# FFN 2 of a macaron layer: quarters' differences taken from PSUM by VectorE, and a pair job's sum taken from its PSUM bank

## The chip, the cores and the metric

The kernel runs on one core of a Trainium2 chip. The metric is the device time of one execution in microseconds. The kernel before takes 1099.75 us, the median of three runs (1099.45 to 1100.01).

The core's engines work side by side, each through its own list of instructions in order, and wait for one another by semaphores: TensorE (PE in the profile) multiplies and writes to PSUM, VectorE (DVE) and ScalarE (ACT) read PSUM and SBUF, GpSimd (POOL) reads SBUF here, and DMAs are issued from SyncE's queue (SP) and POOL's.

## The reference

One layer over 512 tokens of width 1024, in float32: a half-step SwiGLU FFN, a mixer (a recurrent branch and a windowed attention, merged by gates), and a second half-step FFN, each between RMS norms. The part that matters here is the end of the mixer and the first half of FFN 2:

```python
h = h + rms_norm(merged @ w_o[l], mix_post_g[l])
f = swiglu(rms_norm(h, ffn2_pre_g[l]), ffn2_w1[l], ffn2_w3[l], ffn2_w2[l])
h = h + 0.5 * rms_norm(f, ffn2_post_g[l])
```

with `swiglu(x, w1, w3, w2) = (silu(x @ w1) * (x @ w3)) @ w2` and 2816 hidden columns.

## The kernel before

**Precision.** Every float32 operand is held as a high part (a copy rounded to the type float32r) and a low part (what the rounding left), and a product is three matmuls: high by high, high by low, low by high. Making the two parts is called a split here. It is a copy on ScalarE and a subtraction on VectorE (L226 and L227, helper split2): `whi`, `wlo` of weights, `Xh`, `Xl` and the two planes of the tile uT of activations.

**Strassen jobs.** FFN 2's matrix x^T (1024 by 512) lies in quarters: two halves of its features by two halves of its tokens. The first two column tiles of w1 and w3 (128 hidden columns each) are multiplied plainly. The other 20 run in pairs, w1 and w3 in turn: 20 pair jobs (class Pairs, names w1b and w3b, jobs 0 to 19), each with seven block products instead of eight by Winograd's form of Strassen's method. The quarters and four combinations of them are the moving operands:

- b11, b21 and b22 are quarters, as uT holds them;
- t1 = x01 - x00, t2 = x11 - t1, t3 = x11 - x01, t4 = x10 - t2, where x01 is the first half of the features and the second half of the tokens. t1 to t3 are split into slots of SBUF (to_slots), t4 into uT in place of x01 (to_uT).

A job's weights are two raw tiles (a11, a12 and a21, a22). POOL makes the sums S12 (s1, s2) and S34 (s3, s4) of them, four instructions of 512 columns a job (L1038, L1039, L1033, L1034). A job's splits are: the first raw tile, S12, S34 (1024 columns each) and a22 (512). They are made one job ahead, within the previous job: method prep, steps 1 to 4, and step 0 for POOL's sums, two jobs ahead.

**A job's order on PE and what takes its banks.** Each product is 12 matmuls of 128x256. With its three PSUM banks bu, bx and bc a job runs: a11*b11 into bu (copied to q1 by ScalarE, L1083), s1*t1 into bx (copied to q5, L1086), then a22*t4 of the *job before* into that job's own bu, s2*t2 added into bu (copied to u, L1094), a12*b21 into bc (VectorE adds q1, L1106), s4*b22 added into bx (VectorE adds u, L1111), and s3*t3 added into bu. That last sum is the lower right quarter: ScalarE copies bu to v (L1117) and VectorE adds q5 to v (L1118). Then a22*t4 goes on in the same bu, two products later. Every second job (w3) multiplies its results by the silu of those of the job before (L1128, L1129, L1146); the silu (L1141 to L1143) is ScalarE's.

VectorE's order in a job is: split of the next job's first raw tile, split of S12, adds at L1106 and L1111, split of S34, add at L1118, products (in w3's jobs), split of a22.

**The hand-over into FFN 2.** tok_gemm ends the mixer: for each of four tiles of 128 tokens it normalizes, transposes by PE into two PSUM banks (one for each half of the features), and ScalarE and VectorE split the banks into uT (transpose_out, L370 and L372). Beside that, ScalarE copies the unsplit values of all four tiles to four slots xf (transpose_xf, L380), the first two tiles' early, the last two's after the last tile's split. The hook `then` (operands) now runs: a table load for silu, t1 by VectorE from two xf slots and its split, t2 and its split, t3 by POOL; t4 by VectorE (L1998) after it. PE meanwhile multiplies the four plain tiles.

**Slots.** All tiles of SBUF come from one pool of 42 slots, handed out as earlier users release theirs. So what an instruction waits for can be a reader of the slot's earlier tile on any engine.

Of the kernel before, what the change touches and what calls it, by code (L numbers as in the profile page):

```python
# [12 lines left out]
AF = mybir.ActivationFunctionType  # L13
ALU = mybir.AluOpType

P = 128
SEQ = 512
D = 1024
# [8 lines left out]
EPS = 1e-6  # L27
# [24 lines left out]
def hybrid_layer(ctx: ExitStack, tc: tile.TileContext, a: dict, out: bass.AP):  # L52
    nc = tc.nc
    act, dve, pool, pe, sp = nc.scalar, nc.vector, nc.gpsimd, nc.tensor, nc.sync
# [169 lines left out]
    def split2(hi, lo, src):  # L224

        act.activation(hi, src, AF.Copy)  # L226
        dve.tensor_tensor(out=lo, in0=src, in1=f32(hi), op=ALU.subtract)  # L227
# [15 lines left out]
    def unit(nm, i, **kw):  # L243
        w = get(nm, i)
        ps = bank("f")
        mm_feat(ps, w, **kw)
        return ps
# [116 lines left out]
    def transpose_out(banks, t, xf=None, parts=(0, 1)):  # L364
        c = slice(t * P, (t + 1) * P)
        for half, ps in enumerate(banks):
            ks = slice(half * 4, half * 4 + 4)
            v = ps.rearrange("p (k c) -> p k c", k=4)
            if 0 in parts:
                act.activation(uT[:, 0, ks, c], v, AF.Copy)  # L370
            if 1 in parts:
                dve.tensor_tensor(out=uT[:, 1, ks, c], in0=v, in1=f32(uT[:, 0, ks, c]), op=ALU.subtract)  # L372
        if xf:
            transpose_xf(banks, t, xf)

    def transpose_xf(banks, t, xf, halves=(0, 1)):
        for half in halves:
            ps = banks[half]
            v = ps.rearrange("p (k c) -> p k c", k=4)
            act.activation(xf[half, t // 2][:, :, (t % 2) * P : (t % 2 + 1) * P], v, AF.Copy)  # L380


    def tok_gemm(nm, xs, n, R, gpost_name, scale, gpre_name, first, x_to=None, xf=None, spill=False, then=None, eps=D * EPS, pre=None, at_=None, g=None):

# [12 lines left out]
        x_to = x_to or (lambda k: None)  # L397
# [20 lines left out]
        g, us, trs = g or [], {}, {}  # L418
# [122 lines left out]
        t = NT - 1  # L541
# [34 lines left out]
            start(range(1))  # L576
        trs[t] = transpose_mm(us[t])
        transpose_out(trs[t], t)
        transpose_xf(trs[t - 1], t - 1, xf)
        transpose_xf(trs[t], t, xf)  # L580
        if then:
            then()
        if not pre:
# [407 lines left out]
    class Pairs:  # L991
# [75 lines left out]
        def run(self, tail, hooks={}):  # L1067
# [4 lines left out]
            for n, (nm, f) in enumerate(self.jobs):  # L1072
                W = self.w.pop(n)
                first = nm == self.na
                tmp = slot([P, 4, 256], name="ct")
                q1, q5, u, v = (tmp[:, i, :] for i in range(4))
                c = slot([P, 2, SEQ], name="cc")
                if first:
                    self.c1[f] = c
                bu, bx, bc = (bank("c")[:, :256] for _ in range(3))  # L1080
# [33 lines left out]
                silu = lambda: None  # L1114
                mm_s(W["s3"], X["t3"], bu, True)
                del W["s3"], W["s4"]
                act.activation(v, bu, AF.Copy)  # L1117
                dve.tensor_tensor(out=c[:, 1, 256:], in0=v, in1=q5, op=ALU.add)  # L1118
                if n == len(self.jobs) - 1:
                    tail()  # L1120
                    if self.R is not None:
# [214 lines left out]
    ps = [bank("f") for _ in range(NS)]  # L1336
# [385 lines left out]
    for i in range(8):  # L1722
        ps = unit("wg", i)
# [16 lines left out]
    for i in range(2):  # L1740
        ps = unit("wk", i)
# [8 lines left out]
    for t in range(NT):  # L1750
        ps = bank("v")
        c = slice(t * P, (t + 1) * P)
        o = ps[:, :256]
# [20 lines left out]
    for i in range(2):  # L1774
        ps = unit("wq", i)
# [135 lines left out]
    for nm, i in att_units:  # L1911
        w = w_first or get(nm, i)
        w_first = None
        ps = bank("f")
# [32 lines left out]
    hid, tn = Hidden(TAIL_B, GS_B), []  # L1947
    X2 = {"b11": uview(0, 0), "b21": uview(1, 0), "b22": uview(1, 1)}
# [3 lines left out]
    gw = []  # L1952
# [21 lines left out]
    for at_, fn in zip(MARKS_W, (lambda n: split_to(k_w + len(TS_AT) + n + 1), h_back)):  # L1974
        for n, u in enumerate(at_):
            hooks_w[u].append(lambda n=n, fn=fn: fn(n))
    xf = {(hh, th): slot([P, 4, 256], name="xf") for hh in range(2) for th in range(2)}
    def operands():
        act.activation(small(4, "tiny")[:, 0:1], vec[:, 0:1], AF.Silu)
        t = [slot([P, 4, 256], name="T") for _ in range(4)]  # L1980
        tn.extend(t)
        dve.tensor_tensor(out=t[0], in0=xf[0, 1], in1=xf[0, 0], op=ALU.subtract)
        X2["t1"] = to_slots(t[0])
        dve.tensor_tensor(out=t[1], in0=xf[1, 1], in1=t[0], op=ALU.subtract)
        X2["t2"] = to_slots(t[1])
        pool.tensor_tensor(out=t[2], in0=xf[1, 1], in1=xf[0, 1], op=ALU.subtract)
        pairs_b.prep(1, 0)

    rubbish.append(slot([P, D], name="junk"))
    bs = tok_gemm(  # L1990
        "wo", mixed, KT, len(TAIL_W), "mix_post_g", 1.0, "ffn2_pre_g",
        [("w1b", 0), ("w3b", 0), ("w1b", 1), ("w3b", 1)], xf=xf, spill=True, then=operands, eps=4.0 * D * EPS, pre=half_w,
        at_=(0, 2, 3, XW_AT), g=gw)
    half_w = mixed = hooks_w = None
    rubbish.clear()

# [11 lines left out]
    X2 = pairs_b = None  # L2008
# [58 lines left out]
XW_AT = (1, 2, 3, 4)  # L2067
# [59 lines left out]
```

## Time and profile before

| What | Value |
|---|---|
| Median of three runs | 1099.75 us |
| The profiled execution's own time | 1099.81 us |
| Its span, first to last instruction | 1098.0 us |
| Mean granted clock of TensorE | 0.999 |
| First matmul of the pair jobs | 782.1 us after the span's start |
| Busy in 780 to 800 us: PE, DVE, ACT, POOL | 20.00, 19.76, 12.29, 19.68 us |
| Busy in 860 to 880 us: PE, DVE, ACT, POOL | 20.00, 18.71, 10.74, 12.63 us |

The times of the trace count from the start of the span. 1.81 us of the execution lie around the span. A row of a timeline has its start, its duration, engine, line, operation, output and inputs, and in brackets the idle time of the engine ahead of it with what ended that. A duration on VectorE contains the time in which the instruction stands in the engine and does not get on. Matmuls of 256 columns follow each other every 0.12 us and overlap, so their rows are longer (0.28) than their distance.

### The profile page before, as it was taken

How to read it: one execution, taken by the hardware profiler on the slowest of the kernel's cores; microseconds unless marked ns; L12 is line 12 of the kernel's file. 1: busy time of each engine (PE TensorE's matmuls, PEld its weight loads, DVE VectorE, ACT ScalarE, POOL GpSimd, SP SyncE). 2: the span in 40 equal slices, each digit the busy share in tenths (PEclk: the TensorE clock that was granted, in tenths of full speed). 3: DMA queues.
4: the chain of work that ended last, by engine and by line, in shares of the span. 5: the costliest groups of instructions: out<-in, count | busy, mean ns of one | idle time of the engine just before them, and what ended most of it. 6: DMA issues, size and time to landing. Idle time of an engine off the chain costs nothing.

```text
span 1098.0 us, 18217 instructions
## 1 busy us (share of the span) xinstructions
PE 1087.7 (99%) x6880; PEld 986.1 (90%) x6880; DVE 930.4 (85%) x1345; ACT 715.4 (65%) x1241; POOL 405.9 (37%) x366
## 2 busy tenths in 40 slices
PE   9999999999999999999999999999999999999997
PEld 7899999998889878899888888888999999998886
DVE  5987999989997998887778866877899989889996
ACT  7756555598767778666656666457555455578872
POOL 0144933232102613242444443111877656633200
PEclk9999999999999999999999999999999999999999
DMA  9325663389866652156222347676423323449923
GB/s 335 126 84 141 126 154 114 105 189 229 235 166 221 155 156 64 39 192 229 66 90 79 120 138 201 170 254 161 147 78 116 105 88 111 145 102 243 211 74 135
DMA packets 56361, 161.72 MB, mean 147 GB/s; under 512 B 5696, under 2 KB 7616, under 8 KB 56272
## 3 DMA queue, kind: packets, MB, share of 16 engines
q1 hardware_dynamic: 39104, 117.77, 31.7%
q0 software_dynamic: 16880, 42.25, 19.7%
q8 instruction: 54, 0.88, 0.3%
q10 hardware_dynamic: 288, 0.52, 0.1%
q14 instruction: 35, 0.29, 0.1%
HBM read 144.81 MB, written 13.62 MB: 144 GB/s over the span
## 4 chain that ended last, share of the span: by engine, by line
PE 96%; DVE 2%; ACT 1%; issue 1%; DVEq 0%; POOL 0%; ACTq 0%; POOLq 0%
PE c L986 13%; PE c L985 13%; PE c L987 13%; PE f L237 9%; PE f L239 9%; PE f L238 9%; PE hw L857 7%; PE hw L856 7%; PE hw L855 7%; PE pt L1850 1%; PE hw L257 1%; PE hw L255 1%; PE hw L256 1%; PE s L1814 1%; PE s L1813 1%
## 5 line engine op out<-in xcount | busy, mean ns | idle before, releaser
L986 PE MATMUL c<-uT,wlo 128*128 128x256 f32 x516 | 146.1, 283 | 1.3 <-DVE wlo L227 1.3
L987 PE MATMUL c<-uT,whi 128*128 128x256 f32 x516 | 146.0, 283 | 0.0
L985 PE MATMUL c<-uT,whi 128*128 128x256 f32 x516 | 146.0, 283 | 0.0
L986 PE MATMUL c<-Xh,wlo 128*128 128x256 f32 x504 | 142.7, 283 | 0.5 <-DVE wlo L227 0.5
L985 PE MATMUL c<-Xh,whi 128*128 128x256 f32 x504 | 142.7, 283 | 0.0
L237 PE MATMUL f<-uT,whi 128*128 128x512 f32 (+1 forms) x392 | 140.7, 359 | 0.1
L238 PE MATMUL f<-uT,wlo 128*128 128x512 f32 (+1 forms) x392 | 139.1, 355 | 0.0
L239 PE MATMUL f<-uT,whi 128*128 128x512 f32 (+1 forms) x392 | 139.0, 355 | 0.0
L987 PE MATMUL c<-Xl,whi 128*128 128x256 f32 x456 | 129.0, 283 | 0.0
L227 DVE TENSOR_TENSOR wlo<-S,whi 128x1024 fp32r<-128x1024 f32 x86 | 122.5, 1426 | 4.1 <-ACT whi L226 2.0
L226 ACT ACTIVATE whi<-S 128x1024 fp32r<-128x1024 f32 x86 | 88.6, 1055 | 30.4 <-DVE S L1034 28.7
L986 PEld LDWEIGHTS c<-uT,wlo 128*128 128x128 f32 x516 | 99.0, 192 | 1.7 <-DVE wlo L227 1.5
L985 PEld LDWEIGHTS c<-uT,whi 128*128 128x128 f32 x516 | 99.0, 192 | 0.2
L987 PEld LDWEIGHTS c<-uT,whi 128*128 128x128 f32 x516 | 99.0, 192 | 0.0
L986 PEld LDWEIGHTS c<-Xh,wlo 128*128 128x128 f32 x504 | 96.7, 192 | 0.7 <-DVE wlo L227 0.7
L985 PEld LDWEIGHTS c<-Xh,whi 128*128 128x128 f32 x504 | 96.8, 192 | 0.3 <-issue 0.3
L857 PE MATMUL hw<-whi,uT 128*128 128x512 f32 x228 | 88.7, 389 | 0.0
L855 PE MATMUL hw<-whi,uT 128*128 128x512 f32 x228 | 88.7, 389 | 0.0
L987 PEld LDWEIGHTS c<-Xl,whi 128*128 128x128 f32 x456 | 87.5, 192 | 0.0
L237 PEld LDWEIGHTS f<-uT,whi 128*128 128x128 f32 x392 | 74.1, 189 | 11.8 <-issue 1.4
L856 PE MATMUL hw<-wlo,uT 128*128 128x512 f32 x216 | 84.0, 389 | 0.0
L239 PEld LDWEIGHTS f<-uT,whi 128*128 128x128 f32 x392 | 74.1, 189 | 10.5
(453 smaller groups left out, 3202.4 us busy)
## 6 DMA issues: line engine op xcount, KB each, us to landing
raw_w3a<-in_w3a_dram SPq DMA_DIRECT2D x21, 512.0 KB, 4.6
raw_w1a<-in_w1a_dram SPq DMA_DIRECT2D x20, 512.0 KB, 4.4
raw_w1b<-in_w1b_dram SPq DMA_DIRECT2D x20, 512.0 KB, 4.2
raw_w3b<-in_w3b_dram SPq DMA_DIRECT2D x20, 512.0 KB, 4.2
raw_w2a<-in_w2a_dram SPq DMA_DIRECT2D x17, 512.0 KB, 6.5
raw_wg<-in_wg_dram SPq DMA_DIRECT2D x16, 512.0 KB, 3.5
raw_w2a<-in_w2a_dram POOLq DMA_DIRECT2D x15, 512.0 KB, 10.4
raw_w2b<-in_w2b_dram SPq DMA_DIRECT2D x15, 512.0 KB, 8.2
```

Of the source, the lines that this page charges most:

```text
L226: act.activation(hi, src, AF.Copy)
L227: dve.tensor_tensor(out=lo, in0=src, in1=f32(hi), op=ALU.subtract)
L237: pe.matmul(ps[:, c0:c1], wh[:, s], h_, start=k == 0 and c0 == 0, stop=False, skip_group_check=True)
L238: pe.matmul(ps[:, c0:c1], wl[:, s], h_, start=False, stop=False, skip_group_check=True)
L239: pe.matmul(ps[:, c0:c1], wh[:, s], l_, start=False, stop=k == KT - 1, skip_group_check=True)
L255: pe.matmul(acc[n], x[:, 0, c], wh[:, s], start=first, stop=False, skip_group_check=skip)
L855: pe.matmul(ps, xs[:, 0, j, c], hi[:, j, :], start=start and j == 0, stop=False, skip_group_check=True)
L856: pe.matmul(ps, xs[:, 0, j, c], lo[:, j, :], start=False, stop=False, skip_group_check=True)
L857: pe.matmul(ps, xs[:, 1, j, c], hi[:, j, :], start=False, stop=i == self.G - 1, skip_group_check=True)
L985: pe.matmul(ps, wh[:, s], xh, start=first, stop=False, skip_group_check=True)
L986: pe.matmul(ps, wl[:, s], xh, start=False, stop=False, skip_group_check=True)
L987: pe.matmul(ps, wh[:, s], xl, start=False, stop=k == 3, skip_group_check=True)
```

## The change

There are two edits. The first is at the hand-over. The slots xf for the last two token tiles go. tok_gemm gets a hook diff; after the last tile's split, VectorE subtracts straight from the four transposed banks of the last two tiles: t1 from the bank of the first half of the features and x00, t2 from the bank of the second half and t1. t3 is now t2 - x00, the same value, and is made by VectorE instead of POOL. ScalarE's last four copies go. The second is in Pairs.run, for the jobs of FFN 2 alone (self.R is None): no copy to v; VectorE's add reads the bank bu itself.

```diff
+        if diff:
+            diff(t - 1, trs[t - 1])
+            diff(t, trs[t])
+        else:
+            transpose_xf(trs[t - 1], t - 1, xf)
+            transpose_xf(trs[t], t, xf)
...
-                act.activation(v, bu, AF.Copy)
-                dve.tensor_tensor(out=c[:, 1, 256:], in0=v, in1=q5, op=ALU.add)
+                if self.R is not None:
+                    act.activation(v, bu, AF.Copy)
+                dve.tensor_tensor(out=c[:, 1, 256:], in0=bu if self.R is None else v, in1=q5, op=ALU.add)
...
+    xf = {(hh, 0): slot([P, 4, 256], name="xf") for hh in range(2)}
+
+    def differences(t, banks):
+        if not tn:
+            tn.extend(slot([P, 4, 256], name="T") for _ in range(2))
+        c = slice((t % 2) * P, (t % 2 + 1) * P)
+        for o, ps, x in zip(tn, banks, (xf[0, 0], tn[0])):
+            dve.tensor_tensor(out=o[:, :, c], in0=ps.rearrange("p (k c) -> p k c", k=4), in1=x[:, :, c], op=ALU.subtract)
+
     def operands():
         act.activation(small(4, "tiny")[:, 0:1], vec[:, 0:1], AF.Silu)
-        t = [slot([P, 4, 256], name="T") for _ in range(4)]
-        tn.extend(t)
-        dve.tensor_tensor(out=t[0], in0=xf[0, 1], in1=xf[0, 0], op=ALU.subtract)
-        X2["t1"] = to_slots(t[0])
-        dve.tensor_tensor(out=t[1], in0=xf[1, 1], in1=t[0], op=ALU.subtract)
-        X2["t2"] = to_slots(t[1])
-        pool.tensor_tensor(out=t[2], in0=xf[1, 1], in1=xf[0, 1], op=ALU.subtract)
+        X2["t1"] = to_slots(tn[0])
+        tn.extend(slot([P, 4, 256], name="T") for _ in range(2))
+        X2["t2"] = to_slots(tn[1])
+        dve.tensor_tensor(out=tn[2], in0=tn[1], in1=xf[0, 0], op=ALU.subtract)
         pairs_b.prep(1, 0)
```

The line numbers of the changed kernel are higher by 5 in Pairs.run's second half (L1118 becomes L1123).

VectorE at the hand-over, before (T are the combinations t1 to t4, Xl their low parts, hEO the first hidden tiles, the last row the split of job 1's first raw tile):

```order
L1982 TENSOR_TENSOR T_8243<-xf_7673,xf_7672 128x1024
L227 TENSOR_TENSOR Xl_8249<-T_8243,Xh_8248 128x1024
L1984 TENSOR_TENSOR T_8244<-xf_7675,T_8243 128x1024
L227 TENSOR_TENSOR Xl_8254<-T_8244,Xh_8253 128x1024
L1998 TENSOR_TENSOR T_8246<-xf_7674,T_8244 128x1024
L613 TENSOR_TENSOR hEO_8377<-f_8108,sw_8379 128x512
L227 TENSOR_TENSOR Xl_8383<-T_8245,Xh_8382 128x1024
L613 TENSOR_TENSOR hEO_8378<-f_8210,sw_8386 128x512
L227 TENSOR_TENSOR wlo_8390<-raw_w3b_1667_8258,whi_8389 128x1024
```

The same place with the change (tr are the transposed banks):

```order
L1989 TENSOR_TENSOR T_8235<-tr_8119,xf_7672 128x4x128
L1989 TENSOR_TENSOR T_8236<-tr_8124,T_8235 128x4x128
L1989 TENSOR_TENSOR T_8235<-tr_8221,xf_7672 128x4x128
L1989 TENSOR_TENSOR T_8236<-tr_8226,T_8235 128x4x128
L227 TENSOR_TENSOR Xl_8244<-T_8235,Xh_8243 128x1024
L227 TENSOR_TENSOR Xl_8250<-T_8236,Xh_8249 128x1024
L1996 TENSOR_TENSOR T_8247<-T_8236,xf_7672 128x1024
L2008 TENSOR_TENSOR T_8248<-xf_7673,T_8236 128x1024
L617 TENSOR_TENSOR hEO_8373<-f_8106,sw_8375 128x512
L227 TENSOR_TENSOR Xl_8379<-T_8247,Xh_8378 128x1024
L617 TENSOR_TENSOR hEO_8374<-f_8208,sw_8382 128x512
L227 TENSOR_TENSOR wlo_8386<-raw_w3b_1665_8254,whi_8385 128x1024
```

Two differences of 1024 from SBUF have become four of 512 from PSUM, both t1 and t2 stand ahead of the splits, and the difference for t3 has come over from POOL.

PE in job 1, before: the end of s1*t1 and the start of job 0's a22*t4 (c_8395 is job 0's bank bu, w the split of a22), with the semaphores that a row waits for:

```order
L985 MATMUL c_8507<-Xh_8248,whi_8439 128x256
L986 MATMUL c_8507<-Xh_8248,wlo_8440 128x256
L987 MATMUL c_8507<-Xl_8249,whi_8439 128x256
L985 MATMUL c_8395<-uT,w_1616_7979 128x256 [waits Activation_49]
L986 MATMUL c_8395<-uT,w_1616_7979 128x256
```

The same place with the change:

```order
L989 MATMUL c_8502<-Xh_8243,whi_8435 128x256
L990 MATMUL c_8502<-Xh_8243,wlo_8436 128x256
L991 MATMUL c_8502<-Xl_8244,whi_8435 128x256
L989 MATMUL c_8391<-uT,w_1614_7977 128x256 [waits DVE_49]
L990 MATMUL c_8391<-uT,w_1614_7977 128x256
```

The order of the matmuls is the same; a22*t4 waits for VectorE's add where it waited for ScalarE's copy.

POOL's sums of job 3 (the first four rows) and the first of job 4, before:

```order
L1038 TENSOR_TENSOR S_1707_8620<-raw_w3b_1694_8502 128x512 [waits DMAHW5_49,PE_49]
L1039 TENSOR_TENSOR S_1707_8620<-S_1707_8620,raw_w3b_1693_8500 128x512 [waits DMAHW4_49,Pool_49]
L1033 TENSOR_TENSOR S_1708_8621<-raw_w3b_1693_8500,S_1707_8620 128x512 [waits DVE_49,Pool_49]
L1034 TENSOR_TENSOR S_1708_8621<-raw_w3b_1693_8500,raw_w3b_1694_8502 128x512
L1038 TENSOR_TENSOR S_1723_8742<-raw_w1b_1710_8628 128x512 [waits DMAHW7_49,DMASW3_49,DVE_49]
```

The same with the change:

```order
L1042 TENSOR_TENSOR S_1705_8614<-raw_w3b_1692_8497 128x512 [waits DMAHW5_49,PE_49]
L1043 TENSOR_TENSOR S_1705_8614<-S_1705_8614,raw_w3b_1691_8495 128x512 [waits DMAHW4_49,Pool_49]
L1037 TENSOR_TENSOR S_1706_8615<-raw_w3b_1691_8495,S_1705_8614 128x512 [waits DVE_49,Pool_49]
L1038 TENSOR_TENSOR S_1706_8615<-raw_w3b_1691_8495,raw_w3b_1692_8497 128x512
L1042 TENSOR_TENSOR S_1721_8735<-raw_w1b_1708_8622 128x512 [waits DMAHW7_49,PE_49]
```

With two slots fewer in use, the slots have moved on: the first sum of job 4 gets a slot whose last reader is PE (the low part of job 1's first raw tile, read by a12*b21 of job 1), where it was VectorE (the split of job 2's first raw tile).

More of the change, by code (lines that the diff above doesn't have):

```diff
@@ L380, in transpose_xf, with tok_gemm @@
             act.activation(xf[half, t // 2][:, :, (t % 2) * P : (t % 2 + 1) * P], v, AF.Copy)
-    def tok_gemm(nm, xs, n, R, gpost_name, scale, gpre_name, first, x_to=None, xf=None, spill=False, then=None, eps=D * EPS, pre=None, at_=None, g=None):
+    def tok_gemm(nm, xs, n, R, gpost_name, scale, gpre_name, first, x_to=None, xf=None, spill=False, then=None, eps=D * EPS, pre=None, at_=None, g=None, diff=None):
         F = n - R
@@ L578, in tok_gemm @@
         transpose_out(trs[t], t)
-        transpose_xf(trs[t - 1], t - 1, xf)
-        transpose_xf(trs[t], t, xf)
+        if diff:
[4 more added lines that the diff above has]
+            transpose_xf(trs[t], t, xf)
         if then:
@@ L1976, in hybrid_layer @@
             hooks_w[u].append(lambda n=n, fn=fn: fn(n))
-    xf = {(hh, th): slot([P, 4, 256], name="xf") for hh in range(2) for th in range(2)}
+    xf = {(hh, 0): slot([P, 4, 256], name="xf") for hh in range(2)}
[5 more added lines that the diff above has]
+            dve.tensor_tensor(out=o[:, :, c], in0=ps.rearrange("p (k c) -> p k c", k=4), in1=x[:, :, c], op=ALU.subtract)
     def operands():
         act.activation(small(4, "tiny")[:, 0:1], vec[:, 0:1], AF.Silu)
-        t = [slot([P, 4, 256], name="T") for _ in range(4)]
-        tn.extend(t)
-        dve.tensor_tensor(out=t[0], in0=xf[0, 1], in1=xf[0, 0], op=ALU.subtract)
-        X2["t1"] = to_slots(t[0])
-        dve.tensor_tensor(out=t[1], in0=xf[1, 1], in1=t[0], op=ALU.subtract)
-        X2["t2"] = to_slots(t[1])
-        pool.tensor_tensor(out=t[2], in0=xf[1, 1], in1=xf[0, 1], op=ALU.subtract)
+        X2["t1"] = to_slots(tn[0])
+        tn.extend(slot([P, 4, 256], name="T") for _ in range(2))
+        X2["t2"] = to_slots(tn[1])
+        dve.tensor_tensor(out=tn[2], in0=tn[1], in1=xf[0, 0], op=ALU.subtract)
         pairs_b.prep(1, 0)
@@ L1992, in hybrid_layer @@
         [("w1b", 0), ("w3b", 0), ("w1b", 1), ("w3b", 1)], xf=xf, spill=True, then=operands, eps=4.0 * D * EPS, pre=half_w,
-        at_=(0, 2, 3, XW_AT), g=gw)
+        at_=(0, 2, 3, XW_AT), g=gw, diff=differences)
     half_w = mixed = hooks_w = None
```

## The prediction

> **What bounds the kernel now.** I read the page first, then who waits for whom on PE, then each engine's timeline around the pair jobs of FFN 2. The page's head and its line of busy times:
>
> ```profile
> span 1098.0 us, 18217 instructions
> PE 1087.7 (99%) x6880; PEld 986.1 (90%) x6880; DVE 930.4 (85%) x1345; ACT 715.4 (65%) x1241; POOL 405.9 (37%) x366
> ```
>
> TensorE does nearly all of the span, and the change removes no matmul. Time can come only out of PE's waits, or go into new ones. All of them (engine, line, releaser: us in total, times, longest):
>
> ```profile
> PE c L986 <- DVE wlo L227: 1.9, 2, 1.3
> PE w L1305 <- POOL warm L1302: 1.1, 1, 1.1
> PE tr L360 <- DVE hg L350: 0.2, 1, 0.2
> ```
>
> The second is the program's start; the third waits for L350, which stands ahead of every changed instruction. Only the first can be won, two stops at the start of the fourth pair job (PE's timeline; in brackets the idle time ahead of a row and what ended it):
>
> ```profile
> 812.54 0.39 PE L986 MATMUL c<-uT,wlo 128*128 128x256 f32 x1 [1.34 <-DVE wlo L227]
> 814.77 0.39 PE L986 MATMUL c<-Xh,wlo 128*128 128x256 f32 x1 [0.53 <-DVE wlo L227]
> ```
>
> What they cost is read from ScalarE's copy at L1117, which follows the sixth product of every job (jobs 1 to 4, counted from 0):
>
> ```profile
> 801.04 0.39 ACT L1117 ACTIVATE ct<-c 128x256 f32<-128x256 f32 x1 [1.43 <-PE c L987]
> 811.12 0.38 ACT L1117 ACTIVATE ct<-c 128x256 f32<-128x256 f32 x1 [2.04 <-PE c L987]
> 823.58 0.39 ACT L1117 ACTIVATE ct<-c 128x256 f32<-128x256 f32 x1 [1.43 <-PE c L987]
> 833.66 0.39 ACT L1117 ACTIVATE ct<-c 128x256 f32<-128x256 f32 x1 [2.04 <-PE c L987]
> ```
>
> A job takes 10.08 us (seven products of 1.44), job 3 took 12.46: 2.38 us lost, the 1.87 idle and 0.25 for each restart. That is all the change can win.
>
> **Why VectorE is late there.** Rows of VectorE, then of POOL:
>
> ```profile
> 799.41 2.31 DVE L227 TENSOR_TENSOR wlo<-S,whi 128x1024 fp32r<-128x1024 f32 x1
> 801.64 0.41 DVE L1106 TENSOR_TENSOR cc<-c,ct 128x256 f32<-128x256 f32 x1
> 802.31 1.65 DVE L227 TENSOR_TENSOR wlo<-S,whi 128x1024 fp32r<-128x1024 f32 x1
> 803.89 1.52 DVE L1118 TENSOR_TENSOR cc<-ct 128x256 f32<-128x256 f32 x1
> 805.33 1.78 DVE L1128 TENSOR_TENSOR hEO<-cc,cc 128x512 f32<-128x512 f32 x1
> 816.87 0.41 DVE L1118 TENSOR_TENSOR cc<-ct 128x256 f32<-128x256 f32 x1
> 821.23 1.23 DVE L227 TENSOR_TENSOR wlo<-S,whi 128x1024 fp32r<-128x1024 f32 x1
> ```
>
> ```profile
> 800.60 2.28 POOL L1038 TENSOR_TENSOR S<-raw_w1b 128x512 f32<-128x512 f32 x1
> 813.60 2.27 POOL L1034 TENSOR_TENSOR S<-raw_w3b,raw_w3b 128x512 f32<-128x512 f32 x1
> 821.32 2.29 POOL L1038 TENSOR_TENSOR S<-raw_w1b 128x512 f32<-128x512 f32 x1 [5.45 <-DVE wlo L227]
> ```
>
> L1118 takes 0.41 us when POOL is silent (816.87) and 1.52 when POOL works; a split of 1024 takes 1.23 and 2.31. The surcharge is 1.1 us whatever the size: the two engines take turns, and VectorE waits for one POOL instruction. L1106, with one input in PSUM, stays at 0.41 in the same stretch. What PSUM work lies between counts against the turn: after L1106 and L1111 the split waits only 0.43 (1.65).
>
> **The sum at L1118.** Both inputs were in SBUF; one is now the bank. The add then costs 0.41 us at any time, and ScalarE loses 20 copies of 0.39 us (7.8 us), which nothing on PE waited for. By the row 803.89 alone a job of VectorE's shrinks by 1.11 us. But while POOL has work queued, its turn only moves to VectorE's next instruction: what is saved then is the add's own slot in the turns, 0.34, and another 0.34 that now run under POOL's turn, 0.7 a job. [...]
>
> **The sum at the hand-over.** VectorE, ScalarE and POOL between the last transpose and the first split of job 1:
>
> ```profile
> 769.56 1.29 DVE L372 TENSOR_TENSOR uT<-tr,uT 128x512 fp32r<-128x512 f32 x2 [0.24 <-ACT uT L370]
> 771.52 1.23 DVE L1982 TENSOR_TENSOR T<-xf,xf 128x1024 f32<-128x1024 f32 x1 [0.67 <-ACT xf L380]
> 774.47 1.62 DVE L227 TENSOR_TENSOR Xl<-T,Xh 128x1024 fp32r<-128x1024 f32 x1 [1.73 <-ACT Xh L226]
> 779.45 1.23 DVE L227 TENSOR_TENSOR Xl<-T,Xh 128x1024 fp32r<-128x1024 f32 x1 [1.13 <-ACT Xh L226]
> 785.67 1.71 DVE L227 TENSOR_TENSOR wlo<-raw_w3b,whi 128x1024 fp32r<-128x1024 f32 x1
> ```
>
> ```profile
> 769.90 2.08 ACT L380 ACTIVATE xf<-tr 128x512 f32<-128x512 f32 x4
> 771.99 1.28 ACT L1979 ACT_TABLE_LOAD   x1
> ```
>
> ```profile
> 772.06 2.96 POOL L1986 TENSOR_TENSOR T<-xf,xf 128x1024 f32<-128x1024 f32 x1 [10.39 <-DMA raw_w3b<-in_w3b_dram]
> ```
>
> ```profile
> raw_w1b<-in_w1b_dram SPq DMA_DIRECT2D x4, 512.0 KB, 3.9
> ```
>
> ScalarE's 2.08 us go, and its table load moves up under VectorE's work. VectorE gets four differences from PSUM, priced by L372 (same shape and sources, 1.29 for two), with two that wait for the one before: 770.85 to 773.5. The first split T comes at 774.3, the second at 776.5 (each behind a POOL turn). POOL's difference (2.96) becomes one of VectorE's (1.13 and a turn), so POOL starts its sums of job 1 at about 771.6, not 774.99. Its sums of job 2 need a raw tile that lands 3.9 us after an issue at 776.3, so there is a pause in its turns near 780. So the split of 785.67 starts at 784.3, or at 785.4 if that pause isn't there: 0.3 to 1.4 us earlier. VectorE has one instruction more and 3.5 us of idle time less. PE asks for nothing of this before 783.6, the second product of job 0: it is hidden, and would cost only if the differences came 8 us late.
>
> **The new wait.** Until now the product a22*t4, which goes on in the same bank, waited for ScalarE's copy. Now it waits for VectorE's add, which stands behind two or three splits; behind it on PE stands everything. Where it comes (matmuls of the tile c with w, first and last start), and what is around it in jobs 0 and 1:
>
> ```profile
> L985 PE MATMUL c<-uT,w x12: 283/283/283, 793.6 to 817.3; 128*128 128x256 f32 x12
> ```
>
> ```profile
> 790.96 0.39 ACT L1117 ACTIVATE ct<-c 128x256 f32<-128x256 f32 x1 [2.04 <-PE c L987]
> 796.39 1.05 ACT L226 ACTIVATE whi<-raw_w1b 128x1024 fp32r<-128x1024 f32 x1
> ```
>
> ```profile
> 794.02 1.51 DVE L1118 TENSOR_TENSOR cc<-ct 128x256 f32<-128x256 f32 x1
> 797.48 2.00 DVE L227 TENSOR_TENSOR wlo<-raw_w1b,whi 128x1024 fp32r<-128x1024 f32 x1 [0.24 <-ACT whi L226]
> 810.51 1.98 DVE L227 TENSOR_TENSOR wlo<-raw_w3b,whi 128x1024 fp32r<-128x1024 f32 x1
> 812.41 2.31 DVE L227 TENSOR_TENSOR wlo<-S,whi 128x1024 fp32r<-128x1024 f32 x1
> ```
>
> The bank is wanted 2.68 us after L1117's start (793.64 against 790.96): at 793.6, 803.7 and 813.8 for jobs 0, 1, 2. The add of before started at 794.02 and 803.89, too late for both even at 0.41, so all hangs on what comes earlier.
>
> Job 0: from the split's start, the split 1.13, T's split and S12's split 2.23 each with a turn, two PSUM adds 0.67, rest of a turn 0.43, S34's split 1.13, the add 0.41: 8.2 us, so 792.5 (or 793.6): in time, by 1.1 to 0.
>
> Job 1: the first split waits for ScalarE's copy, which ends at 797.44 as before, since it stands behind the job's silu; what was won in job 0 is lost in that wait. But POOL, three microseconds ahead, has by 796.5 done its sums of job 3, and the new order lets it start those of job 4 only when PE has read a tile in job 1's fourth product, at 798.1 (five products after 790.96). Before, it was still behind and surcharged this split: 2.00. So 797.45 + 1.13 + 2.23 + 0.67 + 0.43 + 1.13 + 0.41 = 803.45: in time by 0.25.
>
> Job 2: the products of L1128 and L1129, each with a turn (the first 0.34 less), end at 806.2; the next split at 808.3 instead of 812.49, S12's at 810.5 instead of 814.72. PE wants them at 811.05 and 812.4: both old stops go, with 1.9 us to spare. The add ends at 813.1, wanted at 813.8. From job 3 on the rows with the old duration already leave room; the tightest is job 17:
>
> ```profile
> 964.70 0.39 ACT L1117 ACTIVATE ct<-c 128x256 f32<-128x256 f32 x1 [1.43 <-PE c L987]
> 966.75 1.51 DVE L1118 TENSOR_TENSOR cc<-ct 128x256 f32<-128x256 f32 x1
> ```
>
> 966.75 + 0.41 = 967.16, wanted at 967.4.
>
> Bounds of what the trace does not show: the new wait costs nothing, or 0.75 us at job 1 (its first split surcharged as in the row of 797.48: 0.5 late, 0.25 restart). It can't gain. I take nothing, since POOL's release by PE is an order of instructions, not a duration. Sum: the profiled execution's 1099.81 - 2.38 = 1097.43; the median is 0.06 below that execution, so 1097.4.
>
> [...] The rows 801.64 and 816.87 show 0.41 for both. [...]
>
> **The rivals.** A: the forecast, 1097.0 to 1097.9, chance 0.64. It rests on a margin of 0.25.
>
> B: POOL's turns don't pause where I have them, and the add of job 1 or 2 is late once: 0.75 to 1.4 of the 2.38 come back, 1098.2 to 1098.8. For it: POOL never paused between 772.06 and 815.87 before. Against: the new order ties its sums of job 4 to PE. Chance 0.16.
>
> C: the waits of a22*t4 take just what the others gave back, 1099.8, because POOL takes every turn: late by 0.65 in job 1 and 1.1 in job 2, with two restarts 2.25. Chance 0.08. [...]
>
> D, slower: VectorE's chain isn't earlier in job 0 either. Then the add ends at 794.43 (0.8 late), in job 1 0.6 late, in job 2 1.15, with three restarts 3.3 us for 2.38: 1100.7. It decides as soon as job 0's add ends after 793.65. For it: the rows 794.02 and 803.89. Against: four copies of ScalarE (2.08) and POOL's 2.96 are gone from the chain that VectorE waits in. Chance 0.12, a tail up to 1102.
>
> **How the numbers follow.** The forecast's 1097.4 is the prediction. 1096.9 to 1099.4 holds A and B, 0.8. Two thousandths are 2.2 us, about what a measurement of this kernel can tell from no change; the gain of 2.38 is hardly more. Faster than 1097.55: seven tenths of A, 0.46. Slower than 1101.95: D's tail, 0.06. The rest 0.48 lies within.
>
> **What would show it.** Right: PE's waits hold no row of L227 near 812; the copies' successor, the add, ends before 793.6, 803.7 and 813.8; the split of 785.67 starts near 784.3; job 3 takes 10.08 us; POOL stands still from 796.5 to 798. Wrong: a row of PE's waits for the add on the matmuls of a22*t4, most likely in job 1, or a fourth job still longer than 10.2 us. A time under 1096.8 would mean PE lost time that its waits don't show.

## The result and the profile after

The changed kernel takes 1097.61 us, the median of 18 runs (1097.28 to 1098.15); the kernel before, measured as often beside it, 1099.68. The ratio is 0.9982, 95% interval 0.9975 to 0.9989. The forecast was 1097.4 with a range of 1096.9 to 1099.4.

The page's head and PE's waits follow. The waits are those of before but for one row that is gone:

```profile
span 1095.6 us, 18196 instructions
PE 1087.1 (99%) x6880; PEld 986.2 (90%) x6880; DVE 917.2 (84%) x1348; ACT 705.5 (64%) x1217; POOL 398.8 (36%) x365
```

```profile
PE w L1310 <- POOL warm L1307: 1.1, 1, 1.1
PE tr L360 <- DVE hg L350: 0.3, 1, 0.3
```

Both old stops of job 3 are gone. ScalarE's copy of the first product (L1087) in jobs 2, 3 and 4 shows it; the distances are 10.02 (the first row stands 0.06 late, behind other work) and 10.08 us:

```profile
802.17 0.39 ACT L1087 ACTIVATE ct<-c 128x256 f32<-128x256 f32 x1 [2.42 <-PE c L991]
812.19 0.38 ACT L1087 ACTIVATE ct<-c 128x256 f32<-128x256 f32 x1 [2.96 <-PE c L991]
822.27 0.38 ACT L1087 ACTIVATE ct<-c 128x256 f32<-128x256 f32 x1 [2.36 <-PE c L991]
```

The whole stage can be weighed at once: from the first matmul of the pair jobs to the first behind them, less 140 products of 1.44 (201.60), is what PE lost there. Here are PE's first and last row, and between them a place that the list of waits does not show, the start of job 15's a22*t4, which runs in job 16:

```profile
781.75 0.28 PE L989 MATMUL c<-uT,whi 128*128 128x256 f32 x1
...
944.35 0.28 PE L991 MATMUL c<-Xl,whi 128*128 128x256 f32 x1
944.74 0.39 PE L989 MATMUL c<-uT,w 128*128 128x256 f32 x1
944.96 0.28 PE L990 MATMUL c<-uT,w 128*128 128x256 f32 x1
...
983.72 0.40 PE L859 MATMUL hw<-whi,hx 128*128 128x512 f32 x1
```

983.72 - 781.75 = 201.97, so 0.37 were lost. They lie at 944.74: two steps of 0.39 and 0.22 where 0.12 is usual, 0.27 and 0.10 too much. PE's weight loads, which carry the wait, name VectorE's add as the cause:

```profile
PEld c L989 <- DVE cc L1123: 0.3, 1, 0.3
```

In the trace of before the stage was 986.10 - 782.12 = 203.98, a loss of 2.38, the figure of the prediction. So the stage gained 2.38 and lost 0.37: 2.01, against 2.07 between the medians. (The profiled spans differ by 2.4: the changed kernel's execution came to its pair jobs 0.37 earlier, by chance the same figure as its loss at 944.74. That is no part of the change. In the profiles of the experiments that can be read, the pair jobs begin between 781.62 and 782.30, in no relation to what was edited.)

The rows of VectorE below are the split of job 1's first raw tile, the adds of jobs 0, 1 and 2 (L1123), between them the first split that falls into job 1 (of job 2's first raw tile), and the split of S12 for job 3. Behind them stand POOL's first sums of jobs 1 and 2, its last of job 3 and its first of job 4:

```profile
784.02 1.71 DVE L227 TENSOR_TENSOR wlo<-raw_w3b,whi 128x1024 fp32r<-128x1024 f32 x1
...
792.37 0.41 DVE L1123 TENSOR_TENSOR cc<-c,ct 128x256 f32<-128x256 f32 x1
...
797.10 1.23 DVE L227 TENSOR_TENSOR wlo<-raw_w1b,whi 128x1024 fp32r<-128x1024 f32 x1 [2.95 <-ACT whi L226]
...
802.73 0.41 DVE L1123 TENSOR_TENSOR cc<-c,ct 128x256 f32<-128x256 f32 x1
...
807.94 2.32 DVE L227 TENSOR_TENSOR wlo<-S,whi 128x1024 fp32r<-128x1024 f32 x1
...
812.41 0.41 DVE L1123 TENSOR_TENSOR cc<-c,ct 128x256 f32<-128x256 f32 x1
```

```profile
771.90 1.29 POOL L1042 TENSOR_TENSOR S<-raw_w3b 128x512 f32<-128x512 f32 x1 [10.61 <-issue]
...
780.39 2.03 POOL L1042 TENSOR_TENSOR S<-raw_w1b 128x512 f32<-128x512 f32 x1 [1.35 <-DMA raw_w1b<-in_w1b_dram]
...
795.26 1.29 POOL L1038 TENSOR_TENSOR S<-raw_w3b,raw_w3b 128x512 f32<-128x512 f32 x1
797.72 1.77 POOL L1042 TENSOR_TENSOR S<-raw_w1b 128x512 f32<-128x512 f32 x1 [1.16 <-PE c L990]
```

With 0.37 added for the earlier start, these are the prediction's steps: the split at 784.39 (forecast 784.3), job 1's first split at 797.47, without a turn: 1.23 long (797.45 and, counted to the next instruction's start, 1.13), the adds ending at 793.15, 803.51 and 813.19 (792.5 to 793.6, 803.45 and 813.1), S12's split at 808.31 (first split 808.3, S12's finished 810.5; it ended at 810.63). POOL paused ahead of 780.39 for a raw tile and, in the rows' own times, from 796.55 to 797.72, as forecast. The add of job 1 ends at 803.14, and PE's a22*t4 starts at 803.35: the margin is 0.21 (forecast 0.25).

### The profile page after: what moved, and what is told of

Read it like the earlier page. It is cut to its first block, busy times and chain, and to the rows that moved or that the text cites. A ratio compares the mean times of both kernels' runs of the same rounds, so it can differ in the third digit from the quotient of the medians.

```text
span 1095.6 us, 18196 instructions
## 1 busy us (share of the span) xinstructions
PE 1087.1 (99%) x6880; PEld 986.2 (90%) x6880; DVE 917.2 (84%) x1348; ACT 705.5 (64%) x1217; POOL 398.8 (36%) x365
## 4 chain that ended last, share of the span: by engine, by line
PE 95%; DVE 3%; ACT 1%; issue 1%; DVEq 0%; POOL 0%; ACTq 0%; POOLq 0%
PE c L989 12%; PE c L991 12%; PE c L990 12%; PE f L237 9%; PE f L239 9%; PE f L238 9%; PE hw L859 7%; PE hw L860 7%; PE hw L861 7%; PE pt L1855 1%; DVE wlo L227 1%; PE hw L257 1%; PE hw L255 1%; PE hw L256 1%; PE s L1819 1%
```

## The experiments

My theory after this result: the gain comes from VectorE being early in jobs 0 to 2, and the 0.37 at job 15 is the price of the second edit. Rivals: the shorter add wins; the differences from PSUM win; it is POOL's timing, of which both edits are only carriers. "Lost" below is the stage less 201.60, from each kernel's trace, and a figure in brackets is the 95% interval of the ratio; the medians are of 10 or 11 runs (18 for the first two rows), the difference is to the median of the kernel before on the same chip (1099.68 to 1099.93).

| Kernel | lost in the pair jobs, us | median, us | to before, us | ratio |
|---|---|---|---|---|
| before | 2.38 | 1099.68 | | |
| changed | 0.37 | 1097.61 | -2.07 | 0.9982 (0.9975 to 0.9989) |
| first edit alone | 0.10 | 1097.29 | -2.47 | 0.9980 (0.9971 to 0.9989) |
| second edit alone | 2.27 | 1099.76 | 0.00 | 1.0001 (0.9992 to 1.0010) |
| first edit, t3 on POOL | 2.66 | 1100.34 | +0.62 | 1.0007 (0.9998 to 1.0016) |
| changed, t3 on POOL | 2.87 | 1100.18 | +0.46 | 1.0003 (0.9994 to 1.0012) |
| before, t3 on VectorE | 0.60 | 1098.05 | -1.88 | 0.9984 (0.9975 to 0.9993) |
| before, POOL in halves | 0.00 | 1097.48 | -2.24 | 0.9982 (0.9972 to 0.9991) |
| changed, POOL in halves | 0.06 | 1097.50 | -2.43 | 0.9976 (0.9967 to 0.9985) |
| changed, sums spread | 0.00 | 1097.45 | -2.31 | 0.9978 (0.9970 to 0.9987) |
| first edit, sums spread | 0.00 | 1097.44 | -2.49 | 0.9977 (0.9968 to 0.9987) |
| changed, two adds more | 1.67 | 1099.14 | -0.62 | 0.9994 (0.9985 to 1.0002) |

The loss of the stage less 2.38 gives the difference of the medians within 0.2 us in all rows but one (first edit with t3 on POOL: +0.28 and +0.62; where the other 0.3 are was not found, and the interval of that row is wider than that).

**Which edit? The first alone.** The second edit is taken back:

```diff
-                if self.R is not None:
-                    act.activation(v, bu, AF.Copy)
-                dve.tensor_tensor(out=c[:, 1, 256:], in0=bu if self.R is None else v, in1=q5, op=ALU.add)
+                act.activation(v, bu, AF.Copy)
+                dve.tensor_tensor(out=c[:, 1, 256:], in0=v, in1=q5, op=ALU.add)
```

> The first edit alone: differences from PSUM, t3 by VectorE; ScalarE's copy to v stays and the add reads v. Theory (the gain is VectorE being early enough in jobs 0 to 2, and the late add in job 15 is the price of the second edit): a22*t4 waits for ScalarE again, so job 15 loses nothing (0.37 us that the changed kernel lost there). POOL's sums of job 4 wait for VectorE's split of job 2's first raw tile, so POOL stands still before 798.3 as it does with both edits; the add in job 1 costs 1.5 us again instead of 0.41, and job 3's first split ends near 809.6 where PE wants it at 810.7, S12's near 811.9 where PE wants it at 812.0: both stops still gone, by little. 1097.3 us, up to 1097.8 if one of the two comes late. Rival (both edits are needed, the second for the 0.7 us a job that the prediction counted): a stop of about 1 us stays at job 3, 1098.4 to 1098.8.

Measured 1097.29: the first edit alone has the whole gain, and the theory's number, with S12's split done 1.4 us ahead of its use, where the theory had 0.1. The rows are VectorE's first split in job 1, its add and S12's split for job 3, and POOL's last sum of job 3 and first of job 4:

```profile
797.39 1.23 DVE L227 TENSOR_TENSOR wlo<-raw_w1b,whi 128x1024 fp32r<-128x1024 f32 x1 [1.67 <-ACT whi L226]
...
802.00 1.51 DVE L1122 TENSOR_TENSOR cc<-ct 128x256 f32<-128x256 f32 x1
...
808.65 2.31 DVE L227 TENSOR_TENSOR wlo<-S,whi 128x1024 fp32r<-128x1024 f32 x1
```

```profile
795.14 1.74 POOL L1038 TENSOR_TENSOR S<-raw_w3b,raw_w3b 128x512 f32<-128x512 f32 x1
...
798.70 2.30 POOL L1042 TENSOR_TENSOR S<-raw_w1b 128x512 f32<-128x512 f32 x1 [1.82 <-DVE wlo L227]
```

The add costs 1.51 again, and S12's split is only 0.4 us later than with both edits (0.7 by the rows, 0.3 of it from this execution's later start): PE wanted it by 812.4 here, and it ended at 810.96. POOL's pause is there too, though its sums of job 4 wait for VectorE here and not for PE.

**The second alone.** The hand-over of before, with the add from the bank:

```diff
-                act.activation(v, bu, AF.Copy)
-                dve.tensor_tensor(out=c[:, 1, 256:], in0=v, in1=q5, op=ALU.add)
+                if self.R is not None:
+                    act.activation(v, bu, AF.Copy)
+                dve.tensor_tensor(out=c[:, 1, 256:], in0=bu if self.R is None else v, in1=q5, op=ALU.add)
```

> The second edit alone: no copy to v, VectorE's add reads the bank; the hand-over is that of before. Theory: VectorE is as late in jobs 0 and 1 as before, and now PE waits for its add: in job 0 the add of the trace of before ends at 794.02 + 0.41, 0.8 us after the bank is wanted, in job 1 about 0.6 after, each with 0.1 of restart, and something at job 2 or at the old stops of job 3; with job 15's 0.37 the time is 1100.0 to 1101.2, 1100.6 the likeliest: slower than before. PE's waits hold rows of the add in jobs 0 and 1. Rival (the add's 1.1 us is what wins, the hand-over only decorates): 1098 or less, and no wait for the add in job 0.

Measured 1099.76, no change: 0.2 below the theory's range, and far from the rival. The mechanism is the theory's: PE now stops for the add, in jobs 0 and 1 (in PE's rows, ahead of a22*t4; these are the first two stops of the prediction's rival D) and in job 15.

```profile
794.53 0.39 PE L985 MATMUL c<-uT,w 128*128 128x256 f32 x1 [0.69 <-DVE cc L1119]
...
805.58 0.39 PE L985 MATMUL c<-uT,w 128*128 128x256 f32 x1 [0.71 <-DVE cc L1119]
```

Each costs 0.94 to 0.98 with its restart, job 15 0.37: 2.29 in all. The expectation missed that these stops hold PE back by 1.9 us ahead of job 3, whose old stops of 2.38 then never come. It is a bare exchange. This kernel also settles what moved the wait of POOL's first sum of job 4: by its program's semaphores (POOL doesn't pause there, so no row shows it) that sum waits for PE here too, and with the first edit alone for VectorE. The second edit moved that slot, and not the two slots fewer, as the description of the change has it.

**What in the first edit? t3's engine.** The first edit whole but for one word:

```diff
-        dve.tensor_tensor(out=tn[2], in0=tn[1], in1=xf[0, 0], op=ALU.subtract)
+        pool.tensor_tensor(out=tn[2], in0=tn[1], in1=xf[0, 0], op=ALU.subtract)
```

> The first edit without its move of t3: differences t1 and t2 from PSUM by VectorE, ScalarE's four copies gone, but t3 by POOL; the copy to v stays, so no new wait is there. Theory (POOL's early start carries the gain): VectorE has some microseconds of room in job 0 and loses it in job 1 to ScalarE's copy; POOL is as late as before, every split of job 1 pays its turn, and the stops of job 3 come back nearly whole: 1099.4 us, 1.5 to 2.4 us of them. Rival (the PSUM differences carry it): 1097.3 as with the first edit whole.

Measured 1100.34, 0.9 above the theory: nothing is left of the gain, though the differences still come from PSUM and ScalarE's four copies are still gone. The rows are PE's wait, then POOL's first sum of job 1, its last of job 3, which now runs into job 1's splits, and its first of job 4:

```profile
PE c L990 <- DVE wlo L227: 2.0, 2, 1.5
```

```profile
775.96 2.26 POOL L1042 TENSOR_TENSOR S<-raw_w3b 128x512 f32<-128x512 f32 x1
...
798.36 2.28 POOL L1038 TENSOR_TENSOR S<-raw_w3b,raw_w3b 128x512 f32<-128x512 f32 x1
800.60 2.28 POOL L1042 TENSOR_TENSOR S<-raw_w1b 128x512 f32<-128x512 f32 x1
```

VectorE's rows are those of before nearly to the hundredth from there on: S12's split for job 3 starts at 812.40 (before 812.41). POOL is later than before here: t3 is now made from t2, which VectorE finishes at 773.35, so POOL's first sum of job 1 begins at 775.96 instead of 774.99. What the differences would be worth with POOL just where it was, this run does not show.

The same word in the changed kernel, with both edits:

> The changed kernel with t3 = t2 - x00 made by POOL instead of VectorE, the rest as changed. Theory (what the hand-over wins is POOL's early start: its sums of jobs 1 to 3 begin at 771.9 instead of 775.0, so that POOL is done when job 1's first split comes): POOL makes t3 first, never pauses before job 4's sums, and the first split of job 1, which waits for ScalarE's copy and can't come earlier, takes 2.25 us instead of 1.23; the add of job 1 comes about 0.85 late with 0.1 of restart, as in the run of the second edit alone (0.98 there). The old stops of job 3 stay away, since PE comes 1 us later. With job 15's 0.37: 1098.5 us. Rival (the differences from PSUM and the four copies of ScalarE that are gone carry the gain, t3's place is indifferent): 1097.6.

Measured 1100.18, not to be told from before (its interval holds 1), and 1.7 more than the theory had; its trace loses 0.49 more than the one of before. PE's waits:

```profile
PE c L989 <- DVE cc L1123: 1.6, 2, 1.0
...
PE c L990 <- DVE wlo L227: 0.2, 1, 0.2
```

The add of job 1 comes late (0.83 with its restart; 0.95 expected), and so does that of job 2 (1.26); S12's split for job 3, which the expectation took for safe, is late too (0.46); job 15 has its 0.37. The late adds are those of the prediction's rival C (0.65 in job 1 and 1.1 in job 2, before restarts; measured 0.72 and 1.16), with S12's split and job 15 on top. Rival D's mark, a late add in job 0, does not come: that add ends at 793.21, and PE wants it at 793.63.

And the other way round, the kernel before with t3 alone moved:

```diff
-        pool.tensor_tensor(out=t[2], in0=xf[1, 1], in1=xf[0, 1], op=ALU.subtract)
+        dve.tensor_tensor(out=t[2], in0=xf[1, 1], in1=xf[0, 1], op=ALU.subtract)
```

> The kernel before with one word changed: t3 is subtracted by VectorE instead of POOL, from the two xf slots as before; ScalarE's copies, the differences from SBUF and the copy to v stay. Theory (POOL's early start carries the gain): POOL's sums begin about 3 us earlier; VectorE is 1 us later in job 0, but there is room, and job 1's first split ends near 799.5 without POOL's turn, after which the chain goes as in the run of the first edit alone, 1 us later: S12's split for job 3 ends at 811.9, wanted at 812.4. Both stops gone, 1097.4 us; 1097.9 if one of them stays in part. Rival (VectorE's own chain at the hand-over carries it): one instruction more on VectorE makes the stops longer, 1100 to 1101.

Measured 1098.13, the median of all eleven executions. The profiled one left no trace that can be read; without it the median is 1098.05, and not the 1098.13 that the next expectation gives for the other ten. Either is 0.1 to 0.2 above the theory's range and far from the rival. The kernel was run again:

> The kernel before with t3 subtracted by VectorE instead of POOL and nothing else, once more: the profiled execution of its first run took three times as long with TensorE slow throughout, and can't be read; the other ten took 1098.13 us at the median. Theory (POOL's early start carries the gain, VectorE is 1 us later): 1098.1 again, and the profile shows no stop of 1.3 us at job 3, but what is left of one, 0.5 to 0.9 us in all, at S12's split for job 3 or at a split of job 1. Rival (t3's move wins only part of the stops because POOL still pays turns in job 1): the first stop of job 3 stays with 0.5 or more while POOL's sums of job 4 start before 799.

Measured 1098.05: one word brings 1.88 us, where the first edit brings 2.47 and both edits 2.07. POOL is done with job 3's sums before the second split of job 1, and with job 4's at 806.94, so two of VectorE's splits pay no turn that paid one before: 1.21 and 0.68 us instead of 2.31 and 1.78. What is left of the old stops is 0.46 at S12's split for job 3 (the rest of the 0.60 lies at 784.65 and 942). The row that makes that split late is job 1's first split, which here pays POOL's turn because POOL's sums of job 3 end at 798.19, 1.6 us later than in the changed kernel:

```profile
PE c L986 <- DVE wlo L227: 0.2, 1, 0.2
```

```profile
796.99 2.28 DVE L227 TENSOR_TENSOR wlo<-raw_w1b,whi 128x1024 fp32r<-128x1024 f32 x1
799.19 1.21 DVE L227 TENSOR_TENSOR wlo<-S,whi 128x1024 fp32r<-128x1024 f32 x1
...
807.14 0.68 DVE L227 TENSOR_TENSOR w<-raw_w1b,w 128x512 fp32r<-128x512 f32 x1
```

```profile
796.44 1.75 POOL L1034 TENSOR_TENSOR S<-raw_w3b,raw_w3b 128x512 f32<-128x512 f32 x1
```

So the first edit's other savings at the hand-over, VectorE's and ScalarE's, are worth the rest, about 0.5 us of stage. In the run without t3's move, where POOL is 1 us later than before, they bring nothing.

**Is it POOL's turn as such?** The kernel before with each of POOL's sums made in two instructions of 256 columns (the condition also holds for a few sums of the mixer's pair jobs):

```diff
-                e.tensor_tensor(out=s34[:, :QH], in0=a11, in1=a21, op=ALU.subtract)
+                step = 256 if e is pool and self.R is None else QH
...
+                for o in range(0, QH, step):
+                    e.tensor_tensor(out=s34[:, o : o + step], in0=a11[:, o : o + step], in1=a21[:, o : o + step], op=ALU.subtract)
```

> The kernel before with every sum of POOL for FFN 2's jobs made in two instructions of 256 columns instead of one of 512; the same values. Theory (VectorE stands still for one POOL instruction, so its surcharge has the length of that): the surcharge on VectorE's SBUF operations falls from 1.1 us to 0.5 to 0.7 (a split of 1024 takes 1.7 to 1.9 instead of 2.31, a split of 512 1.2 to 1.4), but POOL, which gets one instruction for each of VectorE's, takes longer for a job's sums. The time is not the test; between 1098 and 1104 by which of the two wins. Rival (the surcharge is a fixed price of 1.1 us for a change of hands, whatever is done in a turn): a split of 1024 still takes 2.3 beside POOL.

Measured 1097.48, below the range expected, with nothing lost in the pair jobs at all: as good as the change, without either of its edits. The rows are VectorE's split and add beside POOL, a pair of POOL's instructions while VectorE waits for something else, and POOL's last pair of job 4:

```profile
799.06 1.76 DVE L227 TENSOR_TENSOR wlo<-S,whi 128x1024 fp32r<-128x1024 f32 x1
...
803.12 0.95 DVE L1124 TENSOR_TENSOR cc<-ct 128x256 f32<-128x256 f32 x1
```

```profile
795.92 1.43 POOL L1043 TENSOR_TENSOR S<-raw_w3b 128x256 f32<-128x256 f32 x2
...
811.86 2.60 POOL L1037 TENSOR_TENSOR S<-raw_w1b,raw_w1b 128x256 f32<-128x256 f32 x2
```

1.76 against 1.21 to 1.23 alone, 0.95 against 0.41: the surcharge is 0.54, and a POOL instruction alone now takes 0.72; with 512 columns they were 1.1 and 1.3. At both lengths the price of a turn is the length of the other engine's instruction less about 0.2 (1.3 - 1.1 and 0.72 - 0.54); it is no fixed price of a change of hands. POOL does fall behind, as the theory had it: its sums of job 4 end at 814.46, where they ended at 808.27 before. But no row of PE's waits follows from it.

**Job 15's late add.** The changed kernel with the four sums of L700 taken apart:

```diff
-            late[end - 4, 1] = [lambda i=i: half.s1(i) for i in range(4)]
+            for i in range(4):
+                late[end - 10 + 2 * i, 1] = [lambda i=i: half.s1(i)]
```

> The changed kernel with the four sums at L700 of job 15 taken apart: one each in jobs 9, 11, 13 and 15, where VectorE waits about 3 us for ScalarE's copy anyway. Theory: job 15's chain starts 5.1 us earlier, its add is in time, and the 0.27 us wait with 0.1 of restart at 944.7 goes: 0.37 less than the changed kernel, 1097.2 us; PE waits for nothing but the start and the 0.3 us at 768. Rival (the wait only moves to job 17, whose add is 0.1 us ahead of its use, or to the jobs that got a sum): within 0.1 us of the changed kernel, 1097.6, with a row of the add in PE's waits elsewhere.

The stop is gone, and the pair jobs take 201.60 us, no loss. The chain starts 2 us earlier and not 5.1, since its first split then waits for ScalarE's copy, and that is enough. The add of job 15 begins at 943.35 instead of 944.27, though this execution's jobs began 0.2 later. First the changed kernel's four sums and its add, then the add of this run:

```profile
933.40 6.88 DVE L700 TENSOR_TENSOR hEO<-hEO,hEO 128x512 f32<-128x512 f32 x4
...
944.27 0.41 DVE L1123 TENSOR_TENSOR cc<-c,ct 128x256 f32<-128x256 f32 x1
```

```profile
943.35 0.41 DVE L1124 TENSOR_TENSOR cc<-c,ct 128x256 f32<-128x256 f32 x1
```

1097.45 us is not to be told from the changed kernel by the medians (0.24 against the expected 0.37, at intervals of 0.9 to either side); the trace carries the verdict. The same spread with the first edit alone:

> The first edit alone, with the four sums of job 15 taken apart over jobs 9, 11, 13 and 15. With the first edit alone PE lost 0.10 us in the pair jobs, at 942 behind those four sums. Theory: that goes, the pair jobs take 201.6 us, the floor of 140 products of 1.44, and no version can gain more there: 1097.2 us, not to be told from the first edit alone. Rival (the sums now delay an add or split elsewhere): a stop in one of jobs 10, 12 and 14, 1097.4 to 1097.8.

No loss, 1097.44. And with POOL's halves in the changed kernel the four sums should shrink too:

> The changed kernel with every sum of POOL for FFN 2's jobs in two instructions of 256 columns, as the kernel before had them in the run that found a surcharge of 0.54 us on VectorE in place of 1.1. Theory (the late add of job 15 is POOL's turns too: four sums of 0.68 us took 1.72 each): the four cost 1.23 each, so job 15's chain starts 2 us earlier and its add is in time; jobs 0 to 2 have more room than in the changed kernel. No row of the add in PE's waits, FFN 2's pair jobs at 201.6 us, 1097.2. Rival (POOL falls behind with twice the turns, so that a sum S34 or S12 comes late for ScalarE's copy, or the add still waits in job 15): 1097.6 or more, with a row for the add or for a split in PE's waits.

Measured 1097.50. The four take 4.66 us instead of 6.88, and job 15 stops no more. One step of PE at 803.6 is 0.07 too long, where the add of job 1 ends only 0.08 ahead of its use. The four sums:

```profile
933.28 4.66 DVE L700 TENSOR_TENSOR hEO<-hEO,hEO 128x512 f32<-128x512 f32 x4
```

**How thin is job 1's margin?** In job 1 alone:

```diff
-                dve.tensor_tensor(out=c[:, 0, 256:], in0=bx, in1=u, op=ALU.add)
+                for _ in range(3 if self.R is None and n == 1 else 1):
+                    dve.tensor_tensor(out=c[:, 0, 256:], in0=bx, in1=u, op=ALU.add)
```

> The changed kernel with the add into c from bx and u made three times in job 1 (the same values again): two instructions of 0.34 us more on VectorE ahead of the S34 split and the add, and nothing else. Theory: the add of job 1 ends 0.15 us ahead of its use, so 0.67 us more makes it 0.5 late, with 0.1 of restart: 0.6 us slower than the changed kernel, 1098.2, with one row of PE's waits for the add in job 1; job 3 stays without stops since its splits had 1.9 us to spare. Rival (POOL's turn that lies behind the two adds absorbs them, as the split of S34 waits for that turn anyway): the first 0.43 of the 0.67 are hidden, 0.1 to 0.3 us slower or nothing.

Measured 1099.14, 1.31 lost in job 1 where 0.6 was expected: both theory and rival fail. VectorE's three adds and the split behind them, and POOL:

```profile
801.02 1.32 DVE L1116 TENSOR_TENSOR cc<-c,ct 128x256 f32<-128x256 f32 x3
802.26 2.11 DVE L227 TENSOR_TENSOR wlo<-S,whi 128x1024 fp32r<-128x1024 f32 x1
```

```profile
799.75 2.16 POOL L1043 TENSOR_TENSOR S<-S,raw_w1b 128x512 f32<-128x512 f32 x1
802.00 1.29 POOL L1037 TENSOR_TENSOR S<-raw_w1b,S 128x512 f32<-128x512 f32 x1
```

The two adds more take 0.45 each, not 0.34 (802.26 - 801.02 = 1.24 for three, 0.34 of it for one alone); each writes where the one ahead of it wrote. And they end after POOL has begun its next instruction at 802.00: the split waits for that one (2.11 instead of the changed kernel's 1.65). So VectorE's PSUM work hid POOL's turn, but it outlasted it, and POOL took another.

## Why the prediction was right, and where not

- **What can be won.** Right: both stops of job 3 went, 2.38 us. What else moved in the stage is job 15's stop, below.
- **The hand-over.** Right where it counts: with the 0.37 added, the four differences end at 773.50 (forecast 773.5) and the split of job 1's first raw tile starts at 784.39 (784.3), and PE waited for none of it. POOL's first sum came 0.7 later than forecast (772.27 against 771.6), and it was still early enough. But the prediction booked POOL's earlier start as one line among others, and it is the term on which most rests: with t3 on POOL the first edit loses 2.66, with t3 moved alone the kernel before loses 0.60.
- **The sum at L1118.** The size held (0.41 in all 20 jobs, 1.51 with the copy and POOL at work). But the step "a job wins 0.7" failed as a part of the gain: the second edit alone wins nothing on the clock, since its wait takes back what it gives, and beside the first edit it costs 0.27 (0.37 against 0.10).
- **The new wait, jobs 0 to 2.** Right: no stop there; the margin of 0.25 in job 1 was there (0.21), and it is thin. The ground given for POOL's pause, that its sums of job 4 are tied to PE, was no ground: with the first edit alone they are tied to VectorE and POOL pauses as well. POOL is done early in both.
- **The new wait, job 3 on.** Wrong. "From job 3 on the rows with the old duration already leave room; the tightest is job 17" was false for job 15, and the trace of before had shown it:

```profile
944.54 0.38 ACT L1117 ACTIVATE ct<-c 128x256 f32<-128x256 f32 x1 [1.43 <-PE c L987]
```

```profile
947.15 0.41 DVE L1118 TENSOR_TENSOR cc<-ct 128x256 f32<-128x256 f32 x1
```

The bank is wanted at 944.54 + 2.68 = 947.22, the add ends at 947.56, 0.34 late with its duration already at 0.41, what the add takes in all 20 jobs with the change. It cost 0.37. What stands ahead of it on VectorE are four sums of FFN 2's last product, placed there when the wait was ScalarE's. Nor was job 17 the tightest of the others: in the trace of before, job 18's add, 0.41 long already, ends only 0.08 ahead of its use (977.38 and 977.46), and job 4's would by the same sum end 0.19 ahead; in the changed kernel both came in time.
- **The time.** 1097.4 forecast, 1097.61 measured: with job 15's term the sum would have been 1099.68 - 2.38 + 0.37 = 1097.67. The range held partly by luck: the overlooked stop was small, and the gain wrongly given to the add could not show, because the first edit alone already wins all of job 3's 2.38.
- **The rivals.** B did not come in jobs 0 to 2; its kind came once, at job 15, for half its price. C's time, the new waits taking back what the others gave, is what the second edit does alone (1099.76), but by stops in jobs 0, 1 and 15; the first two of these are D's. C's stops, in jobs 1 and 2, came with both edits and t3 back on POOL, where they and two more lose 2.87.

## What to carry to other kernels

When a wait is handed from an idle engine to a busy one, check every instance of it against its use, one by one, and not only where the busy engine is known to be late: the odd one out here was a job with foreign work hooked in. Where two engines take turns, as VectorE and POOL do here (in the trace of before a split of 1024 took 1.23 us while POOL was silent and 2.31 with a turn of POOL's), ask first when the other engine is done, and only then what each instruction costs: here, POOL's sums starting three microseconds earlier (771.58 with t3 alone moved, 774.99 before) were worth more, 1.88 us, than all that was taken off VectorE, the late engine, about 0.5 together with ScalarE's copies. And the length of the other engine's instruction is a knob of its own: halving it (a surcharge of 0.54 us instead of 1.1) did here, by itself, what the change did (1097.48 and 1097.61).

Four versions come to the floor of the pair jobs, three exactly and one within 0.06 us (first edit or both with the sums spread, halves without and with the change); between 1097.44 and 1097.50 no measurement of this kernel tells them apart.

## What the runs showed of the hardware

- VectorE's surcharge beside POOL was 1.1 us where POOL's instructions had 512 columns (before: a split of 1024 took 2.31 instead of 1.23) and 0.54 where they had 256 (before with POOL in halves: 1.76 instead of 1.21 to 1.23).
- With two adds more, an add of VectorE that repeats the one ahead of it, to the same place, took 0.45 us instead of 0.34; why, no run here shows.
- A stop of PE cost 0.10 us more than the wait, in the step behind it (0.22 or 0.23 instead of 0.12), at each of the 15 stops of 0.2 us or more in the pair jobs of these traces (before 2, changed 1, second edit alone 3, first edit with t3 on POOL 2, changed with t3 on POOL 4, before with t3 on VectorE 1, two adds more 2). The changed kernel's stop of 0.27 us at 944.74 is in no row of PE's waits; the weight loads' waits (0.3) and the steps between matmuls (0.39 and 0.22) show it.
